# Masks of the transposed attention scores: added by VectorE in PSUM in place of matmuls with an identity

## The chip, the cores and the metric

The kernel runs on one core of one Trainium2 chip. The metric is the device time of one execution in microseconds (us); smaller is better. A "profile" here is one execution recorded by the hardware profiler: its span runs from the first to the last instruction that it lists.

## The reference, cut to what matters

One layer of a hybrid decoder trunk over 1024 tokens, 1024 wide, in float32. The input is normalised and projected once; four head groups of 256 channels work on the projection: sparse attention with three branches (NSA), differential attention, retention, and a Mamba-2 scan. Their outputs are gated, concatenated and projected back. The change touches the two attentions, whose scores are masked before the exponential:

```
def masked_softmax(s, mask):
    s = jnp.where(mask, s, -jnp.inf)
    m = jnp.max(s, axis=-1, keepdims=True)
    p = jnp.exp(s - jnp.where(jnp.isfinite(m), m, 0.0))
    return p / jnp.maximum(jnp.sum(p, axis=-1, keepdims=True), 1e-30)
...
dist = tb[:, None] - tk[None, :]                        # differential attention, per 128 queries
p = masked_softmax(s - slopes * dist, dist >= 0)         # causal
...
mask = (dist >= 0) & (dist < WINDOW) & (tk[:, None, :] >= 0)   # NSA window branch, WINDOW = 512
```

## The kernel before, in words

All matmuls of the projections and of the attention split one operand into a high and a low part (float32r) and accumulate several products in PSUM. `proj_t` (lines 267 to 269) and `proj_n` (283 to 285) issue three matmuls per block of 128 inputs; `weights` loads and splits the weights (254 on ScalarE, 187 in `low` on GpSimd).

Each attention head is computed twice over 512 queries (u = 0, 1). A first pass has queries on partitions: `diff_rows` and `nsa_rows` compute score tiles (helper `scores`, line 173), `Stats.tile` adds the mask and takes the maximum on VectorE in place in PSUM (476; 474 without a mask), ScalarE takes the exponential and the sum (477), and `Stats.shifts` and `rows` turn the sums into one shift per query, which is stored as extra rows of the query operand. A second pass has keys on partitions: `diff_out` and `nsa_out` compute the transposed scores, which now come out already shifted. For each block kb of 128 keys the score tile `S` is one or two matmuls (173 and, for NSA, 1079). Where the block meets the diagonal, or in the window branch its far edge, a 128-column mask is added. In the kernel before this is one more matmul into the same accumulation: the identity in bf16 as weights, the mask in bf16 (0 or -3e38) as the moving operand. It stands at line 582 in `score_t` (differential attention, tiles wider than 256 columns, one per softmax map), at 621 in `diff_out` (both maps in one tile of 2 x 256, the mask repeated for both), and at 1083 in `nsa_out` (one branch in a tile, or two narrow branches in one tile, again repeated). Then ScalarE takes the exponential from PSUM (`e`, lines 631, 623, 1088), the probabilities are split (`pth`, `ptl`: 589 and 592 in `pv`, 1090 to 1094 in `nsa_out`), and two matmuls multiply them with V into `O` (593, 594, 1098).

PSUM tiles come from rings: three buffers `S` for all score tiles, one `O`, two `mm` for projections, two `R` for the rest:

```
PSB = dict(S=3, O=1, mm=2, R=2)
```

Three streams of work are written as generators, each of whose steps issues a few instructions: `attention`, `recurrent` (`ssd_group`, `ret_pair`) and `projections`, which ends with `ssm_rows`, `ret_rows`, `gated`, `out_partial` (1203 to 1205, 1225) and `out_final`. `merge` picks the next step by weights (attention 400, recurrence 70, projections 660); attention and recurrence are lifted in priority. A scheduler then fixes every engine's order at build time, by priority and by its own estimate of when an instruction can start; on the chip each engine runs its list in that order.

```
att_, rec_ = lifted(attention(), PRIO), lifted(recurrent(), PRIO)
merge((att_, W_ATT), (rec_, W_REC), (proj, W_PROJ))
```

Of the kernel before, what the change touches and what calls it, by code (L numbers as in the profile page):

```python
# [15 lines left out]
ALU = mybir.AluOpType  # L16
# [6 lines left out]
P = 128  # L23
# [100 lines left out]
def hybrid_trunk_kernel(ctx: ExitStack, tc: tile.TileContext, a, out, dbg=None):  # L124
    nc = tc.nc
    V, A, T, G, SP = nc.vector, nc.scalar, nc.tensor, nc.gpsimd, nc.sync
# [14 lines left out]
    def sb(tag, shape, dt=F32):  # L141
        uid[0] += 1
        name = f"{tag}{uid[0]}"
        if tag == "w":
            return wpieces.pop(0)
        if tag in rings:
            return rings[tag].tile(shape, dt, name=name, padded_shape=[P] + list(shape[1:]))
        assert slots[tag], tag + " has no free slot"
        s = slots[tag].pop(0)
        t = s.tile(shape, dt, name=name)  # L150
        held[t.tensor.name] = (tag, s)
        return t

    def free(*tiles):
        for t in tiles:
            tag, s = held.pop(t.tensor.name)
            slots[tag].append(s)

    def const(name, shape, dt=F32):
        return pool.tile(shape, dt, name=name, tag=name, bufs=1)  # L160
# [4 lines left out]
    def ps(tag, shape):  # L165
        uid[0] += 1
        return psum.tile(shape, F32, name=f"{tag}{uid[0]}", tag=PMAP[tag], bufs=PSB[PMAP[tag]])
# [3 lines left out]
    def scores(tile_, *args, **kw):  # L171

        ins = T.matmul(tile_, *args, **kw)  # L173
        if kw["start"]:
            pace.append(ins)
# [18 lines left out]
    x = a["x"][0]  # L194
# [170 lines left out]
    m_causal_t, m_lower_t = [mk[:, i * P:(i + 1) * P] for i in (5, 6)]  # L365
    m_cmp = mk[:, 7 * P:7 * P + 512]
    ident_bf = const("ident_bf", [P, P], BF16)
# [42 lines left out]
    qa, ka, vd = {}, {}, {}  # L410
# [114 lines left out]
    def pair(m):  # L525

        return m[:, None, :].to_broadcast([P, 2, P])
# [12 lines left out]
    def diff_rows(h, u):  # L540
# [30 lines left out]
            move(qa[h, m][98:100, 512 * u:512 * u + 512], d_sd[h][u][2 * m:2 * m + 2, :])  # L571
        yield

    def score_t(s, w, parts, mask_lo, mask_hi):

        last = len(parts) - 1
        masks = [m for m in (mask_lo, mask_hi) if m is not None]
        for n, (k, q) in enumerate(parts):
            scores(s[:k.shape[-1], :q.shape[-1]], k, q, start=(n == 0), stop=(n == last and not masks))
        for n, (c, mk_) in enumerate(masks):  # L580
            kk = parts[0][0].shape[-1]
            T.matmul(s[:kk, c:c + mk_.shape[-1]], ident_bf[:kk, :kk], mk_, start=False, stop=(n == len(masks) - 1))

    def pv(o, e, vv, c0, w, first, last, hi_eng):

# [10 lines left out]
    def halves(dst, o):  # L596

        A.activation(dst, o[64:128, :], AF.Copy)
        V.tensor_tensor(dst, o[0:64, :], dst, op=ALU.add)

    def wide(q, lo, hi):

        a = min(lo, hi - 256)
        return q[:, a:hi], lo - a

    def diff_out(h, u):
        j, h2 = divmod(h, 2)
        if h2 == 0 and u == 0:
            y_diff[j] = sb("b", [P, S])
        o = ps("O", [P, 512])  # L610
        nk = 4 * u + 4
        for kb in range(nk):
            lo, hi = max(512 * u, kb * P), 512 * u + 512
            w = hi - lo
            es = []
            if w <= 256:
                s = ps("S", [P, 2, 256])
                for m in range(2):
                    q, x0 = wide(qa[h, m][0:100], lo, hi)
                    scores(s[:, m, :], ka[h, m][0:100, kb * P:kb * P + P], q, start=(m == 0), stop=False)  # L620
                T.matmul(s[:, :, x0:x0 + P], ident_bf, pair(m_causal_t), start=False, stop=True)
                e = sb("e", [P, 2, 256])
                A.activation(e[:, :, :w], s[:, :, x0:], AF.Exp)
                es = [e[:, 0, :w], e[:, 1, :w]]
            for m in range(2 if w > 256 else 0):
                s = ps("S", [P, 512])
                q, x0 = wide(qa[h, m][0:100], lo, hi)
                score_t(s, w, [(ka[h, m][0:100, kb * P:kb * P + P], q)],
                        (x0, m_causal_t) if kb * P >= 512 * u else None, None)
                e = sb("e", [P, 512])  # L630
                A.activation(e[:, :w], s[:, x0:x0 + w], AF.Exp)  # L631
                es.append(e[:, :w])
            V.scalar_tensor_tensor(es[0], es[1], neglam, es[0], op0=ALU.mult, op1=ALU.add)
            pv(o, es[0], vd[h][:, kb, :], lo - 512 * u, w, kb == 0, kb == nk - 1, A)
            yield
        halves(y_diff[j][64 * h2:64 * h2 + 64, 512 * u:512 * u + 512], o)
        yield
        if u:
            free(qa[h, 0], qa[h, 1], ka[h, 0], ka[h, 1], vd[h])
        if h2:  # L640
            diff_finish(j, u)
            yield
# [404 lines left out]
    def nsa_out(h, u):  # L1047
        hp, h2 = divmod(h, 2)
        if h2 == 0 and u == 0:
            y_nsa[hp] = sb("b", [P, S])  # L1050
        us = slice(512 * u, 512 * u + 512)
        o = ps("O", [P, 512])
        s = ps("S", [P, 2, P])
        for j in range(2):
            T.transpose(s[:, j, :], e_cmp[h, u][:, j, :], ident)
        hl = [sb(n, [P, 2, P], F32R) for n in ("pth", "ptl")]
        split(hl[0], hl[1], s)
        for a in range(2):
            for i in range(2):
                T.matmul(o[:, 256 * a:256 * a + 256], vvc[:, a, :], hl[i].rearrange("p j c -> p (j c)"),  # L1060
                         start=(a + i == 0), stop=False)
        yield
        groups, small = [], []
        for kb in range(4 * u + 4):
            for b in ("win", "slc"):
                lo, hi = max(512 * u, kb * P), 512 * u + 512
                edge = b == "win" and kb * P + 5 * P <= hi
                if edge:
                    hi = kb * P + 5 * P
                (small if hi - lo <= 256 else groups).append((b, kb, lo, hi, edge))  # L1070
        groups = [[g] for g in groups] + [small[i:i + 2] for i in range(0, len(small), 2)]
        for gi, g in enumerate(groups):
            wb = 256 if len(g) == 2 else 512
            s = ps("S", [P, len(g), wb])
            for j, (b, kb, lo, hi, edge) in enumerate(g):
                a0 = min(lo, hi - 256)
                scores(s[:, j, :hi - a0], k1[b][:, kb * P:kb * P + P], q1[h][:, a0:hi], start=(j == 0), stop=False)
                diag = kb * P >= 512 * u
                T.matmul(s[:, j, :hi - a0], k2[b][0:72, kb * P:kb * P + P], q2[h][0:72, a0:hi], start=False,
                         stop=not (edge or diag) and j == len(g) - 1)  # L1080
            for on, x, m in ((diag, lo - a0, m_causal_t), (edge, hi - a0 - P, m_lower_t)):
                if on:
                    T.matmul(s[:, :, x:x + P], ident_bf, m[:, None, :].to_broadcast([P, len(g), P]), start=False,  # L1083
                             stop=m is m_lower_t or not edge)
            xa, xb = min(e[2] - min(e[2], e[3] - 256) for e in g), hi - a0
            e, hl = sb("e", [P, len(g), wb]), [sb(n, [P, len(g), wb], F32R) for n in ("pth", "ptl")]
            e, hl = e[:, :, :xb - xa], [t[:, :, :xb - xa] for t in hl]
            A.activation(e, s[:, :, xa:xb], AF.Exp)  # L1088
            if gi % LO_POOL == LO_POOL - 1:
                A.activation(hl[0], e, AF.Copy)  # L1090
                G.tensor_tensor(hl[1], e, hl[0].bitcast(F32), op=ALU.subtract)
            else:
                G.tensor_scalar(hl[0], e, 1.0, 1.0, op0=ALU.mult, op1=ALU.mult)  # L1093
                V.tensor_tensor(hl[1], e, hl[0].bitcast(F32), op=ALU.subtract)  # L1094
            for j, (b, kb, lo, hi, edge) in enumerate(g):
                x = lo - min(lo, hi - 256) - xa
                for i, t in enumerate(hl):
                    T.matmul(o[:, lo - 512 * u:hi - 512 * u], vvs[b][:, kb, :], t[:, j, x:x + hi - lo], start=False,  # L1098
                             stop=(g is groups[-1] and j + i == 2))
            yield  # L1100
        halves(y_nsa[hp][64 * h2:64 * h2 + 64, us], o)
        yield
        if u:
            free(q1[h], q2[h])
            if h == 3:
                for b in ("win", "slc"):
                    free(k1[b], k2[b], vvs[b])
# [341 lines left out]
```

## Time and profile before

| what | value |
|---|---|
| three runs | 765.43, 770.51, 770.57 us; median 770.51 |
| profiled execution | 773.71 us, of it 771.9 us span |
| mean granted TensorE clock | 0.984 of full speed |
| TensorE busy (matmuls) | 727.9 us, 94% |
| TensorE weight loads | 591.7 us, 77%, beside the matmuls |
| VectorE busy | 509.2 us, 66%, 1452 instructions |
| ScalarE busy | 413.7 us, 54% |
| GpSimd busy | 305.3 us, 40% |

PE is TensorE's matmuls, PEld its weight loads, DVE is VectorE, ACT ScalarE, POOL GpSimd. A busy share is a mean over stages: what a stage costs is read from the stretch in which it stands. Successive matmuls overlap in the records, so the distance between their starts tells more than their length.

### The profile page before, as it was taken

What the parts mean: (1) busy time and instruction counts of PE and PEld (TensorE: products, weight loads), DVE (VectorE), ACT (ScalarE), POOL (GpSimd) and SP (SyncE); (2) the same over time, 40 slices, a digit from 0 to 9 for tenths busy, and PEclk for the clock granted to TensorE, in tenths of its full rate; (3) what the DMA queues carried; (4) which work ended last, traced back from release to release, by engine and by line L of the source; (5) the groups of instructions that cost most, each with busy time, mean ns of one, the idle gap of its engine ahead of it and who ended that gap; (6) DMA issues with size and microseconds to landing.
All of it is one profiled execution on the core that took longest, in us unless ns stands there. A gap on an engine that the chain in (4) does not pass through costs nothing.

```text
span 771.9 us, 12391 instructions
## 1 busy us (share of the span) xinstructions
PE 727.9 (94%) x3876; PEld 591.7 (77%) x3876; DVE 509.2 (66%) x1452; ACT 413.7 (54%) x1029; POOL 305.3 (40%) x476
## 2 busy tenths in 40 slices
PE   4999999999999999997999999999978999999994
PEld 4888777767787898775889888778866778788773
DVE  3752566444866856685696856657679897435587
ACT  6721566455667765473565544444446664454354
POOL 4231227111123115332442464456557752352446
PEclk9999999999999999999999999999987999999998
DMA  8548647755532533453232743225364223334365
GB/s 277 165 141 241 180 128 188 226 151 161 147 90 84 143 102 90 110 157 107 82 103 71 167 113 77 79 81 152 85 191 135 68 87 114 109 132 142 110 259 191
DMA packets 100845, 104.91 MB, mean 136 GB/s; under 512 B 15234, under 2 KB 76236, under 8 KB 100764
## 3 DMA queue, kind: packets, MB, share of 16 engines
q1 hardware_dynamic: 100684, 103.77, 45.8%
q8 instruction: 30, 0.49, 0.3%
q14 instruction: 35, 0.29, 0.2%
q0 software_dynamic: 96, 0.36, 0.1%
HBM read 71.91 MB, written 32.54 MB: 135 GB/s over the span
## 4 chain that ended last, share of the span: by engine, by line
PE 56%; DVE 14%; DMA 13%; issue 7%; POOL 5%; ACT 3%; SPq 1%; DVEq 0%; POOLq 0%; ACTq 0%
PE mm L267 7%; PE mm L268 7%; PE mm L269 7%; PE S L173 6%; DMA t<-d_cs 4%; PE mm L284 3%; PE mm L283 3%; PE mm L285 3%; PE O L1098 2%; DMA wraw<-in_w_in_dram 2%; POOL wlo L187 2%; DMA b<-in_w_in_dram 2%; DVE ptl L1094 2%; PE R L943 1%; PE mm L1203 1%
## 5 line engine op out<-in xcount | busy, mean ns | idle before, releaser
L187 POOL TENSOR_TENSOR wlo<-wraw,whi 128x256 fp32r<-128x256 f32 x132 | 99.3, 782 | 178.9 <-ACT whi L254 150.0
L267 PE MATMUL mm<-h,whi 128*128 128x512 f32 x400 | 161.9, 406 | 0.7 <-ACT ev L292 0.4
L268 PE MATMUL mm<-h,wlo 128*128 128x512 f32 x400 | 160.5, 401 | 0.0
L269 PE MATMUL mm<-h,whi 128*128 128x512 f32 x400 | 160.0, 400 | 0.0
L477 ACT ACTIVATE S<-S,sj 128x512 f32<-128x512 f32 (+3 forms) x192 | 103.7, 540 | 89.4 <-DVE sj L476 65.7
L173 PE MATMUL S<-b,b 100*128 100x256 f32 (+5 forms) x384 | 132.2, 366 | 6.7 <-ACT S L477 4.5
L476 DVE CUSTOM_DVE_ANT_0 S<-S,mk 128x512 f32<-128x512 f32 (+3 forms) x144 | 70.3, 495 | 40.5 <-PE S L173 17.1
L173 PEld LDWEIGHTS S<-b,b 100*128 100x128 f32 (+1 forms) x384 | 72.3, 192 | 23.7 <-ACT S L477 8.5
L267 PEld LDWEIGHTS mm<-h,whi 128*128 128x128 f32 x400 | 76.1, 190 | 16.2 <-ACT ev L292 0.6
L269 PEld LDWEIGHTS mm<-h,whi 128*128 128x128 f32 x400 | 75.9, 190 | 15.1
L268 PEld LDWEIGHTS mm<-h,wlo 128*128 128x128 f32 x400 | 75.9, 190 | 14.3 <-POOL wlo L187 0.4
L1093 POOL TENSOR_SCALAR pth<-e 128x512 fp32r<-128x512 f32 (+2 forms) x64 | 38.9, 613 | 56.3 <-ACT e L1088 25.8
L283 PE MATMUL mm<-whi,h 128*128 128x256 f32 (+1 forms) x192 | 55.8, 292 | 0.6 <-DVE ssmb L679 0.6
L1094 DVE TENSOR_TENSOR ptl<-e,pth 128x512 fp32r<-128x512 f32 (+2 forms) x64 | 45.7, 722 | 15.9 <-POOL pth L1093 13.4
L284 PE MATMUL mm<-wlo,h 128*128 128x256 f32 (+1 forms) x192 | 55.8, 293 | 0.0
L1088 ACT ACTIVATE e<-S 128x512 f32<-128x512 f32 (+2 forms) x76 | 40.3, 542 | 26.2 <-PE S L1083 14.7
L285 PE MATMUL mm<-whi,h 128*128 128x256 f32 (+1 forms) x192 | 54.2, 288 | 0.0
L254 ACT ACTIVATE whi<-wraw 128x1024 fp32r<-128x1024 f32 x29 | 30.6, 1055 | 24.4 <-DMA wraw<-in_w_in_dram 23.3
L474 DVE TENSOR_REDUCE sj<-S 128x1 f32<-128x512 f32 x48 | 32.6, 684 | 15.5 <-PE S L173 12.4
L631 ACT ACTIVATE e<-S 128x512 f32<-128x512 f32 (+1 forms) x64 | 35.7, 568 | 12.7 <-PE S L173 8.4
L778 DVE SCALAR_TENSOR_TENSOR t<-t,ncs,t 128x128 f32<-128x128 f32 x32 | 14.1, 475 | 38.8 <-POOL t L775 38.7
L477 ACT ACTIVATION_READ_ACCUMULATOR S<-S,sj 128x1 f32 x192 | 37.8, 197 | 0.0
(325 smaller groups left out, 1710.6 us busy)
## 6 DMA issues: line engine op xcount, KB each, us to landing
wraw<-in_w_in_dram SPq DMA_DIRECT2D x27, 512.0 KB
b<-in_x_dram SPq DMA_DIRECT2D x8, 512.0 KB
t<-d_cs SPq DMA_DIRECT2D x32, 128.0 KB
wraw<-in_w_out_dram SPq DMA_DIRECT2D x16, 256.0 KB
ev<-in_x_dram SPq DMA_DIRECT2D x16, 256.0 KB
d_part<-ev SPq DMA_DIRECT2D x16, 256.0 KB
b<-d_part SPq DMA_DIRECT2D x8, 512.0 KB
out_dram<-b SPq DMA_DIRECT2D x16, 256.0 KB
```

Source lines behind the costliest of these rows:

```text
L173: ins = T.matmul(tile_, *args, **kw)
L187: G.tensor_tensor(dst[:, cs], src[:, cs], hi[:, cs].bitcast(F32), op=ALU.subtract)
L267: paced(T.matmul(p, w[k][0], h_hi[k][:, hs], start=(k == 0), stop=False))
L268: T.matmul(p, w[k][1], h_hi[k][:, hs], start=False, stop=False)
L269: T.matmul(p, w[k][0], h_lo[k][:, hs], start=False, stop=(k == NK - 1))
L283: paced(T.matmul(p, h_hi[k][:, hs], w[k][0], start=(k == 0), stop=False))
L284: T.matmul(p, h_hi[k][:, hs], w[k][1], start=False, stop=False)
L285: T.matmul(p, h_lo[k][:, hs], w[k][0], start=False, stop=(k == NK - 1))
L476: V.tensor_tensor_reduce(s, s, bound, -1.0, -NEG, ALU.add, ALU.min, nm)
L477: A.activation(s, s, AF.Exp, bias=nm, scale=1.0 if bound is None else -1.0, accum_out=self.d[:, b, i, c:c + 1])
L1088: A.activation(e, s[:, :, xa:xb], AF.Exp)
L1094: V.tensor_tensor(hl[1], e, hl[0].bitcast(F32), op=ALU.subtract)
```

## The change

The 108 matmuls with the identity, and their weight loads, are gone. The last score matmul closes the accumulation (`stop`), and VectorE adds the mask to the tile in PSUM in place, before ScalarE reads it. Nothing else is edited; `nsa_rows` keeps its own mask matmul at line 988 and `ident_bf` with it.

```
+    def masked(s, m):
+        V.tensor_tensor(s, s, m, op=ALU.add)
...
     def score_t(s, w, parts, mask_lo, mask_hi):
         last = len(parts) - 1
-        masks = [m for m in (mask_lo, mask_hi) if m is not None]
         for n, (k, q) in enumerate(parts):
-            scores(s[:k.shape[-1], :q.shape[-1]], k, q, start=(n == 0), stop=(n == last and not masks))
-        for n, (c, mk_) in enumerate(masks):
-            kk = parts[0][0].shape[-1]
-            T.matmul(s[:kk, c:c + mk_.shape[-1]], ident_bf[:kk, :kk], mk_, start=False, stop=(n == len(masks) - 1))
+            scores(s[:k.shape[-1], :q.shape[-1]], k, q, start=(n == 0), stop=(n == last))
+        for c, mk_ in (m for m in (mask_lo, mask_hi) if m is not None):
+            masked(s[:parts[0][0].shape[-1], c:c + mk_.shape[-1]], mk_)
...
-                    scores(s[:, m, :], ka[h, m][0:100, kb * P:kb * P + P], q, start=(m == 0), stop=False)
-                T.matmul(s[:, :, x0:x0 + P], ident_bf, pair(m_causal_t), start=False, stop=True)
+                    scores(s[:, m, :], ka[h, m][0:100, kb * P:kb * P + P], q, start=(m == 0), stop=(m == 1))
+                masked(s[:, :, x0:x0 + P], pair(m_causal_t))
...
-                         stop=not (edge or diag) and j == len(g) - 1)
+                         stop=j == len(g) - 1)
             for on, x, m in ((diag, lo - a0, m_causal_t), (edge, hi - a0 - P, m_lower_t)):
                 if on:
-                    T.matmul(s[:, :, x:x + P], ident_bf, m[:, None, :].to_broadcast([P, len(g), P]), start=False,
-                             stop=m is m_lower_t or not edge)
+                    masked(s[:, :, x:x + P], m[:, None, :].to_broadcast([P, len(g), P]))
```

In the lists of the engines' orders, a name is a program name with the number of its tile; lines are those of the kernel listed. On TensorE, at the first masked tile of the differential attention (head 0, first half, `S_1348`), the difference of the two orders reads (- before only):

```order
 L269 MATMUL mm_1279<-h_164,whi_1272 128x512
 L173 MATMUL S_1348<-b_849,b_850 128x512
-L582 LDWEIGHTS ident_bf
-L582 MATMUL S_1348<-mk,ident_bf 128x128
 L267 MATMUL mm_1279<-h_157,whi_1272 128x512
 L268 MATMUL mm_1279<-h_157,wlo_1273 128x512
```

The load of the identity and the mask are gone; the projection matmuls around the score keep their places.

On VectorE, at the same place, while the shifts of another tile (`sj_1068`, the `Stats.shifts` of the second half) are worked out, the order before is:

```order
L492 TENSOR_TENSOR sj_1068<-sj_1068 128x16
L493 TENSOR_TENSOR sj_1068<-sj_1068 128x8
L496 TENSOR_SCALAR sj_1068<-sj_1068 128x8
L443 CAST sj_1068<-sj_1068 128x8
L444 TENSOR_SCALAR sj_1068<-sj_1068 128x8
L446 TENSOR_TENSOR sj_1068<-sj_1068 128x8
L447 TENSOR_SCALAR sj_1068<-sj_1068 128x8
L448 RECIPROCAL sj_1068<-sj_1068 128x8
L449 SCALAR_TENSOR_TENSOR sj_1068<-sj_1068 128x8
L633 SCALAR_TENSOR_TENSOR e_1351<-e_1356,lam,e_1351 128x512
```

And of the changed kernel, where line 576 is the new addition and 635 is the former 633:

```order
L576 TENSOR_TENSOR S_1348<-S_1348,mk 128x128
L492 TENSOR_TENSOR sj_1068<-sj_1068 128x16
L493 TENSOR_TENSOR sj_1068<-sj_1068 128x8
L496 TENSOR_SCALAR sj_1068<-sj_1068 128x8
L443 CAST sj_1068<-sj_1068 128x8
L444 TENSOR_SCALAR sj_1068<-sj_1068 128x8
L446 TENSOR_TENSOR sj_1068<-sj_1068 128x8
L576 TENSOR_TENSOR S_1353<-S_1353,mk 128x128
L447 TENSOR_SCALAR sj_1068<-sj_1068 128x8
L448 RECIPROCAL sj_1068<-sj_1068 128x8
L449 SCALAR_TENSOR_TENSOR sj_1068<-sj_1068 128x8
L450 TENSOR_TENSOR sj_1068<-sj_1068 128x8
```

The additions for the two maps now stand among the small steps of the statistics, and the combination of the two maps comes behind both.

Late in the program, on VectorE, where the second half of the SSM rows is normalised (`h_7057`, `sm_7062`) and the window and compressed scores of later NSA heads are on their way, the order before is:

```order
L1165 SCALAR_TENSOR_TENSOR h_6097<-PT_6981,vec,h_6096 128x512
L998 TENSOR_REDUCE sj_7198<-S_7227 128x4
L476 ISA S_7260,sj_7198<-S_7260,mk 128x128
L476 ISA sj_7198 128x1
L231 TENSOR_SCALAR sm_6871<-sm_6871 128x2
L231 TENSOR_SCALAR sm_7062<-sm_7062 128x4
```

And of the changed kernel (lines behind 577 are one or two higher than before: 1129 is the former 1128, 1166 the former 1165, 1157 the former 1156):

```order
L576 TENSOR_TENSOR S_7133<-S_7133,mk 128x128
L859 TENSOR_REDUCE sm_6871<-u_6870 128x2
L488 TENSOR_TENSOR sj_6558<-sj_6558 128x12
L231 TENSOR_SCALAR sm_7062<-sm_7062 128x4
L1129 SCALAR_TENSOR_TENSOR ev_6997<-PT_6992,wret,ev_6997 128x512
L231 TENSOR_SCALAR sm_6871<-sm_6871 128x2
L489 TENSOR_SCALAR sj_6558<-sj_6558 128x12
L576 TENSOR_TENSOR S_7180<-S_7180,mk 128x128
L1166 SCALAR_TENSOR_TENSOR h_6097<-PT_6981,vec,h_6096 128x512
L490 TENSOR_TENSOR sj_6558<-sj_6558 128x24
L1157 TENSOR_TENSOR h_7057<-h_7057,sm_7062 128x1024
```

Two additions stand between the steps that make the SSM rows ready for the output projection, and the normalisation of these rows comes earlier against the statistics of the attention.

## Rows read from the trace of the kernel before

**Rows 1.** The page, busy time: us, share of the span, instructions.

```profile
PE 727.9 (94%) x3876; PEld 591.7 (77%) x3876; DVE 509.2 (66%) x1452; ACT 413.7 (54%) x1029; POOL 305.3 (40%) x476
```

**Rows 2.** Busy time by stretch: length, engines, then clock, DMA share, GB/s.

```profile
0.00:325.00 325.00, 310.33 (x1636) 251.97 (x1637) 195.38 (x572) 185.67 (x446) 94.50 (x151) 1.00 0.55 156
325.00:375.00 50.00, 43.90 (x215) 34.52 (x214) 33.39 (x100) 25.81 (x63) 17.10 (x29) 0.97 0.43 116
375.00:550.00 175.00, 173.54 (x1015) 145.06 (x1014) 122.59 (x396) 90.19 (x232) 82.98 (x142) 1.00 0.38 102
550.00:650.00 100.00, 89.96 (x485) 72.12 (x484) 87.57 (x254) 56.93 (x160) 58.05 (x90) 0.93 0.38 117
650.00:775.00 125.00, 110.16 (x533) 88.00 (x532) 70.32 (x134) 55.06 (x130) 52.65 (x66) 0.96 0.42 152
```

**Rows 3.** The same view, engines PE PEld DVE ACT POOL, two shorter stretches.

```profile
571.50:594.00 22.50, 18.45 (x75) 13.68 (x75) 22.26 (x62) 14.74 (x43) 16.95 (x26) 0.70 0.59 185
612.50:637.00 24.50, 22.59 (x142) 18.77 (x142) 23.84 (x68) 15.39 (x43) 13.26 (x19) 1.00 0.33 106
```

**Rows 4.** Groups by line and shape: the mask matmuls; count, busy us, mean ns.

```profile
L1083 PE MATMUL S<-mk,ident_bf 128*128 128x128 bf16 x40 | 9.3, 233 | 0.0
L582 PE MATMUL S<-mk,ident_bf 128*128 128x128 bf16 x32 | 7.4, 231 | 0.0
L1083 PE MATMUL S<-mk,ident_bf 128*128 128x256 bf16 x20 | 5.5, 284 | 0.0
L621 PE MATMUL S<-mk,ident_bf 128*128 128x256 bf16 x16 | 4.5, 284 | 0.0
```

**Rows 5.** Timeline of TensorE around two masks: start us, length us, instruction.

```profile
112.95 0.23 PE L582 MATMUL S<-mk,ident_bf 128*128 128x128 bf16 x1
112.99 0.48 PE L267 MATMUL mm<-h,whi 128*128 128x512 f32 x1
113.30 0.39 PE L268 MATMUL mm<-h,wlo 128*128 128x512 f32 x1
113.54 0.39 PE L269 MATMUL mm<-h,whi 128*128 128x512 f32 x1
...
186.84 0.28 PE L621 MATMUL S<-mk,ident_bf 128*128 128x256 bf16 x1
186.88 0.48 PE L268 MATMUL mm<-h,wlo 128*128 128x512 f32 x1
187.19 0.39 PE L269 MATMUL mm<-h,whi 128*128 128x512 f32 x1
```

**Rows 6.** Mask matmuls by stretch (PE, PEld): lines 582, 621, then 1083 thrice.

```profile
325.00:375.00 50.00, 1.39 (x6) 0.58 (x6) 0.97 0.43 116
325.00:375.00 50.00, 1.14 (x4) 0.39 (x4) 0.97 0.43 116
550.00:650.00 100.00, 4.23 (x17) 1.62 (x17) 0.93 0.38 117
571.50:594.00 22.50, 0.80 (x3) 0.34 (x3) 0.70 0.59 185
612.50:637.00 24.50, 1.49 (x6) 0.58 (x6) 1.00 0.33 106
```

**Rows 7.** Groups by line and shape: VectorE's bounded maximum in PSUM, two widths.

```profile
L476 DVE CUSTOM_DVE_ANT_0 S<-S,mk 128x128 f32<-128x128 f32 x44 | 12.9, 293 | 9.8 <-PE S L1034 6.1 <-PE S L173 1.5 <-ACT S L477 1.4
L476 DVE CUSTOM_DVE_ANT_0 S<-S,mk 128x256 f32<-128x256 f32 x28 | 11.9, 427 | 5.8 <-ACT S L477 2.7 <-PE S L1034 2.2 <-PE S L173 0.5
```

**Rows 8.** Waits of all engines: waited for; us in total, times, longest.

```profile
ACT S L477 <- DVE sj L476: 65.7, 69, 3.7
```

**Rows 9.** Waits of TensorE alone.

```profile
PE S L173 <- ACT S L477: 4.5, 5, 2.5
PE O L1098 <- DVE ptl L1094: 2.8, 6, 0.8
```

**Rows 10.** Timeline of TensorE: one matmul and the idle time before it.

```profile
571.55 0.33 PE L994 MATMUL S<-tri,t 128*128 128x128 f32 x1 [2.66 <-ACT t L990]
```

## The prediction

> **What bounds the kernel now.** I read the share of busy time first, then the busy time by stretch, then what TensorE waits for, then the two stretches where it waits most, and last the single instructions that the change swaps. TensorE is busy 727.9 of the 771.9 us span, VectorE 509.2 [rows 1]. By stretch the picture splits [rows 2]: up to 325 us TensorE works 310.33 of 325 us (most of what is missing is the start), from 375 to 550 us 173.54 of 175, with VectorE at 60 to 70%. There, time is TensorE's own work, and what another engine does beside it is covered. From 325 to 375 us TensorE works 43.90 of 50 and from 550 to 650 us 89.96 of 100; in the latter VectorE works 87.57. Inside it are two pieces, 571.5 to 594 and 612.5 to 637 us, where VectorE is full (22.26 of 22.50 and 23.84 of 24.50) while TensorE is not (18.45 and 22.59) [rows 3]. I read these 47 us as VectorE's: by the code, the last recurrence chunks, the rows of the SSM and retention outputs, the statistics of the next attention rows and the split of the probabilities come together there, and the partial output projection, which would fill TensorE, starts only behind them. After 650 us TensorE works 110.16 us again and VectorE 70.32 [rows 2]; the end is the tail of the final normalisation, which the change does not touch.
>
> **What goes from TensorE.** The removed instructions are 32 + 16 in the differential attention and 40 + 20 in the NSA attention: 72 over 128 columns and 36 over 256, each with its own weight load of the identity [rows 4]. Their durations (231 to 284 ns) overlap with their neighbours, so what counts is how far one moves the next starts. Matmuls of 512 columns normally start 0.23 to 0.24 us apart (113.30 to 113.54). After a 128-column mask the second matmul starts at 113.30 instead of 112.95 + 0.23 = 113.18: the mask costs 0.12 us. After a 256-column mask it starts at 187.19 instead of 186.84 + 0.23 = 187.07: again 0.12 us [rows 5]. So all 108 take 108 x 0.12 = 13.0 us of TensorE, and this is the most the removal can give.
>
> [...]
>
> What of this lies on the path? Of the 108, 6 + 4 stand between 325 and 375 us and 17 between 550 and 650 us, 3 and 6 of them in the two pieces that VectorE fills [rows 6]. The other 108 - 10 - 17 = 81, and the 8 of the 17 outside the two pieces, stand where TensorE is the longest: 89 x 0.12 = 10.7 us gained. The 9 in the full pieces gain nothing, since TensorE waits there anyway.
>
> **What comes to VectorE.** 108 in-place additions, PSUM and a bf16 mask to PSUM. The trace has no plain one, but VectorE's bounded maximum of line 476 reads a score tile in PSUM and a bf16 mask and writes the tile back: 293 ns for 128 columns, 427 for 256 [rows 7]. I take these: 72 x 0.293 + 36 x 0.427 = 36.5 us, VectorE at 545.7 us in all, still below TensorE's 714.9.
> - In the dense stretches (81 of them, some 27 us) the additions run beside projection matmuls. I cost them at nothing: VectorE has 30 to 40% free there. Were that cover gone, each would show with its whole 0.34 us on average.
> - In the two full pieces they cost their duration. By the times of before 9 masks fall there, two of them wide (1.49 us for the second piece's six is 4 x 0.233 + 2 x 0.284 [rows 4, 6]): 7 x 0.293 + 2 x 0.427 = 2.9 us. By the instruction order of the changed program, 18 additions (12 narrow, 6 wide) stand on VectorE between the first gated row and the first partial output: 12 x 0.293 + 6 x 0.427 = 6.1 us. I take the middle, 4.5.
> - Between 325 and 375 us ten masks come: 6 x 0.293 + 4 x 0.427 = 3.5 us of VectorE in a stretch where it is 67% busy and TensorE idles 6.1 us. At worst all 3.5 show; at best the ten matmuls gain 10 x 0.12 = 1.2. I take 1.0 lost, nearer to the gain, since VectorE is not full.
>
> **The added hop.** Exp now waits for VectorE instead of TensorE, so one of the three S buffers stays taken longer, and behind a waiting addition on VectorE stand the small statistics and the split of the probabilities, for which TensorE's products with V wait. The nearest thing in the trace is the row path: 144 tiles go TensorE, VectorE (line 476), ScalarE (line 477) through the same three buffers. ScalarE waited 65.7 us for VectorE on this path [rows 8], yet TensorE waited only 4.5 us for a buffer, and 2.8 us for the split [rows 9]: 4.5 / 144 = 0.03 us a tile. For 108 tiles that would be 3.4 us, but most of the 4.5 lies in the full pieces, which are already counted; I take 0, with 0 and 3.4 as ends.
>
> No DMA is added, removed or newly waited for: SyncE's list holds the same transfers in nearly the same order. The order on TensorE keeps its pattern, masks taken out, with products with V and recurrence steps a few matmuls earlier or later.
>
> **Sum.** -10.7 + 4.5 + 1.0 + 0 = -5.2 us. The profiled execution took 773.7 us, so 768.5; it lies 3.2 us above the median of the runs shown, 770.5. From the median the forecast is 765.3 us, 0.7% faster. A difference under 1% (7.7 us) is about what a measurement of this kernel cannot tell from none, so the likeliest verdict is "within 1%".
>
> **Rivals.**
> 1. *All of TensorE's gain is kept.* VectorE's pieces are full because work is queued, not because it must all be done there: after the pieces, from 650 us on, VectorE is busy for little more than half of the time [rows 2], and additions could displace work that nobody waits for. Then the 89 give 10.7, the ten 1.2: 770.5 - 11.9 = 758.6 us. Against it: VectorE is busy 97 to 99% in the pieces [rows 3], and attention, with its masks, has the higher priority in the order. It is faster by over 1% as soon as the two VectorE losses together stay below 3.0 us.
> 2. *VectorE's queue becomes the wait.* One mechanism: the addition stands in program order behind whatever VectorE does, so a masked tile holds its S buffer for its own 0.34 us plus one VectorE instruction (509.2 us / 1452 = 0.35 us), 0.69 us more, and TensorE, whose order is fixed, stands at the next score matmul. If that shows for every third mask, 36 x 0.69 = 24.8 us against 13.0 gained: 770.5 + 11.8 = 782.3 us. It decides from 13.0 / 108 = 0.12 us a mask for no gain, and from (13.0 + 7.7) / 108 = 0.19 us a mask for slower by 1%. For it: the 65.7 us of ScalarE's waits. Against it: TensorE's 0.03 us a tile. [...]
> 3. *Gain and loss cancel.* The full pieces take all 6.1, the stretch from 325 us all 3.5: -10.7 + 9.6 = -1.1, 769.4 us. Within 1%, as the forecast.
>
> **How the numbers follow.** Forecast and rival 3 together 0.48, rival 1 0.31, rival 2 0.21. Rival 1's end with everything hidden is -13.0 us, 757.5; below that I see nothing. Above, 779 leaves out somewhat over half of rival 2, under 0.2. Faster by over 1% is below 762.8, slower above 778.2.
>
> **What would show it.** Right: 108 fewer matmuls on TensorE, its busy time down by 8 to 13 us; 108 VectorE additions near 0.29 and 0.43 us; TensorE as dense as before up to 325 us and from 375 to 550 us, with the score's next stages some 10 us earlier by 550 us; and the 47 us of VectorE's pieces grown by 3 to 6. Wrong: TensorE's waits for ScalarE's exp or for the split of the probabilities grown by 10 us or more, a drop of the granted clock in a stretch that was dense, additions that take much over 0.45 us, or the full pieces not longer at all.

## The result, and the profile after

The changed kernel takes 759.03 us (median of four runs, 757.33 to 764.18) against 770.54 us of the kernel before in the same comparison: a ratio of 0.985, with a 95% interval of 0.982 to 0.989. It is faster by 1.5%, and the interval lies wholly below 1. The forecast was 765.3 us and "within 1%"; the measured time is that of rival 1 (758.6 us). The experiments below show a second thing: the 1.5% belongs to one instruction order, and four other orders of the same instructions do not have it. One profiled execution among them (the kernel before at weight 655) ran at a mean granted clock of 0.845 and took 797.02 us, so its parts are not used.

The page of the changed kernel, busy times over a span of 757.1 us (before: [rows 1]):

```profile
PE 715.2 (94%) x3768; PEld 591.7 (78%) x3768; DVE 528.9 (70%) x1560; ACT 415.0 (55%) x1029; POOL 312.6 (41%) x476
```

108 matmuls fewer and 108 VectorE instructions more, as the diff says. TensorE is busy 12.7 us less, VectorE 19.7 us more. Its additions, as groups by line and shape (count, busy us, mean ns, then the idle time before them):

```profile
L576 DVE TENSOR_TENSOR S<-S,mk 128x128 f32<-128x128 f32 x72 | 20.8, 292 | 10.6 <-PE S L173 6.2 <-PE S L1081 3.8
L576 DVE TENSOR_TENSOR S<-S,mk 128x256 f32<-128x256 f32 x36 | 15.4, 431 | 7.1 <-PE S L1081 5.6 <-ACT u L837 0.8 <-PE S L173 0.4
```

292 and 431 ns, beside the 293 and 427 ns that were assumed from the bounded maximum [rows 7]: 36.2 us in all. VectorE's busy time has grown by only 19.7 us, though: successive records overlap on VectorE too. Before, the durations of its 1452 instructions add up to 590.4 us at a busy time of 509.2; after, those of 1560 add up to 618.7 at 528.9. So the overlap grew by 8.6 us (81.2 to 89.8), and the durations of the 1452 other instructions add up to some 8 us less than before (618.7 less 36.6 for the additions, beside 590.4). By stretch (length, the engines in the order of the page, clock, DMA share, GB/s; before: [rows 2]):

```profile
0.00:325.00 325.00, 308.93 (x1624) 254.95 (x1625) 205.64 (x613) 189.84 (x455) 97.46 (x154) 1.00 0.55 156
325.00:375.00 50.00, 47.99 (x241) 39.88 (x241) 37.13 (x128) 27.47 (x68) 18.57 (x32) 0.97 0.48 131
375.00:550.00 175.00, 172.42 (x999) 146.52 (x997) 130.37 (x412) 91.78 (x236) 89.36 (x146) 1.00 0.42 114
550.00:650.00 100.00, 91.93 (x469) 73.60 (x470) 85.14 (x267) 56.22 (x157) 57.23 (x85) 0.95 0.35 107
650.00:775.00 125.00, 93.94 (x440) 76.75 (x438) 70.64 (x143) 49.70 (x115) 49.93 (x63) 0.95 0.38 135
```

The stretch from 325 to 375 us, for which a loss of 1.0 us was forecast, is denser than before: TensorE idles 50 - 47.99 = 2.0 us there in place of 6.1. Two landmarks say more than fixed times. The last projection matmul (line 267) starts at 544.6 us, before at 568.0: 23.4 us earlier. Up to there TensorE has this behind it, first of the kernel before, then of the changed one:

```profile
0.00:568.03 568.03, 545.62 (x2963) 446.33 (x2964) 362.44 (x1098) 309.06 (x761) 201.47 (x335) 1.00 0.48 135
0.00:544.62 544.62, 525.23 (x2842) 438.83 (x2843) 368.70 (x1138) 304.26 (x744) 200.91 (x324) 1.00 0.50 140
```

Of the 121 matmuls fewer, 69 are masks (32 of line 582, 16 of 621, 21 of 1083); the other 52 (net) have moved behind the last projection matmul. The second landmark is the 24th matmul at the former line 1203. (By the code each tile of the output projection has six of them, so 24 are four tiles; the expectations below call this place the eighth output tile.) It starts at 633.2 us, before at 646.6: 13.4 earlier, so the late stretch between the two has grown by 10.0 us. From there to the end it is 123.9 us, before 125.3. The late stretch, in the same columns, of the kernel before:

```profile
568.00:646.60 78.60, 68.75 (x366) 54.46 (x365) 73.19 (x209) 48.60 (x136) 51.04 (x76) 0.91 0.36 112
```

and of the changed kernel:

```profile
544.60:633.20 88.60, 79.27 (x413) 62.31 (x412) 81.53 (x260) 54.55 (x154) 58.37 (x85) 0.94 0.35 106
```

It is longer because more of the program stands in it, 413 matmuls in place of 366, and TensorE works 10.5 us more; it idles 9.3 us in it, before 9.9. VectorE is 92% busy in it, before 93%, with 17 of the additions (5.8 us) among its work. So TensorE's waiting in the stretch that VectorE nearly fills did not grow under the additions.

For an account of the whole span I take three parts from the profile: TensorE's idle time (span less busy time), the half-clock loss (half of TensorE's busy time in stretches with a granted clock of 0.5), and the rest, its work at full clock. The half is an estimate: in the changed kernel's stretch at 346 us below, matmuls of 512 columns start 0.43 us apart, just ahead of it 0.23. The second part comes from the stretches with a clock of 0.5. Of the kernel before they are:

```profile
351.50:354.90 3.40, 3.40 (x10) 2.63 (x10) 1.92 (x3) 0.61 (x2) 2.62 (x4) 0.50 0.03 12
573.40:587.00 13.60, 10.82 (x34) 7.83 (x33) 13.50 (x38) 7.83 (x25) 11.32 (x18) 0.50 0.79 251
764.50:771.90 7.40, 0.00 (x0) 0.00 (x0) 3.24 (x4) 1.18 (x3) 3.01 (x4) 0.50 0.55 208
```

and of the changed kernel:

```profile
346.20:349.60 3.40, 3.40 (x10) 2.60 (x9) 1.33 (x4) 1.97 (x4) 0.67 (x1) 0.51 0.64 171
551.00:561.20 10.20, 9.18 (x35) 7.80 (x36) 9.40 (x31) 5.37 (x17) 9.16 (x14) 0.50 0.64 202
714.90:718.30 3.40, 3.40 (x11) 2.83 (x12) 3.03 (x6) 1.99 (x4) 1.55 (x3) 0.50 0.00 0
749.00:757.10 8.10, 0.00 (x0) 0.00 (x0) 3.24 (x4) 1.27 (x3) 3.10 (x4) 0.50 0.51 194
```

Before, (3.40 + 10.82) / 2 = 7.1 us are lost to the clock; after, (3.40 + 9.18 + 3.40) / 2 = 8.0.

| us | span | work at full clock | half-clock loss | idle |
|---|---|---|---|---|
| before | 771.9 | 720.8 | 7.1 | 44.0 |
| after | 757.1 | 707.2 | 8.0 | 41.9 |
| difference | -14.8 | -13.6 | +0.9 | -2.1 |

In these two executions the saved work is all kept. They differ by more than the medians, 14.9 us beside 11.5, since that of the kernel before lies 3.2 us above its median; by the medians 2.1 of the 13.6 us came back. One execution's waiting is thus known to a few us only (the kernel before took 767.61 to 773.57 us in 25 runs of one comparison). Waits of all engines (waited for; us in total, times, longest): ScalarE's wait for VectorE on the row path is 48.5 us, before 65.7 [rows 8], and 32.9 us of waits for the additions have come beside it:

```profile
ACT S L477 <- DVE sj L476: 48.5, 55, 4.1
ACT e L1089 <- DVE S L576: 19.8, 19, 2.8
ACT e L633 <- DVE S L576: 8.6, 15, 1.6
ACT e L625 <- DVE S L576: 4.5, 5, 2.0
```

The largest of TensorE's own waits for a score buffer and for the split probabilities are 3.2 and 4.0 us, before 4.5 and 2.8 [rows 9]; with all smaller ones of either kind they are 3.8 and 5.1, before 4.7 and 5.1:

```profile
PE O L1099 <- DVE ptl L1095: 4.0, 7, 1.3
PE S L173 <- ACT S L477: 3.2, 4, 1.6
```

### The profile page after: what moved, and what is told of

It is laid out like the page before. It is cut to its first block, busy times and chain, and to the rows that moved or that the text cites. A ratio compares the mean times of both kernels' runs of the same rounds, so it can differ in the third digit from the quotient of the medians.

```text
span 757.1 us, 12299 instructions
## 1 busy us (share of the span) xinstructions
PE 715.2 (94%) x3768; PEld 591.7 (78%) x3768; DVE 528.9 (70%) x1560; ACT 415.0 (55%) x1029; POOL 312.6 (41%) x476
## 4 chain that ended last, share of the span: by engine, by line
PE 63%; DMA 14%; DVE 11%; POOL 5%; issue 3%; ACT 2%; SPq 1%; DVEq 0%; POOLq 0%; ACTq 0%
PE mm L267 9%; PE mm L269 9%; PE mm L268 9%; PE S L173 7%; DMA t<-d_cs 4%; PE O L1099 3%; PE mm L284 2%; PE mm L283 2%; PE mm L285 2%; DMA b<-in_w_in_dram 2%; PE mm L1206 1%; PE mm L1204 1%; PE mm L1205 1%; PE S L1081 1%; PE R L945 1%
## 5 line engine op out<-in xcount | busy, mean ns | idle before, releaser
L477 ACT ACTIVATE S<-S,sj 128x512 f32<-128x512 f32 (+3 forms) x192 | 103.4, 539 | 75.7 <-DVE sj L476 48.5
L173 PE MATMUL S<-b,b 100*128 100x256 f32 (+5 forms) x384 | 130.5, 363 | 4.5 <-ACT S L477 3.2
L268 PEld LDWEIGHTS mm<-h,wlo 128*128 128x128 f32 x400 | 75.9, 190 | 14.9
L576 DVE TENSOR_TENSOR S<-S,mk 128x128 f32<-128x128 f32 (+1 forms) x108 | 36.2, 339 | 17.7 <-PE S L1081 9.4
L474 DVE TENSOR_REDUCE sj<-S 128x1 f32<-128x512 f32 x48 | 32.6, 684 | 15.1 <-PE S L173 10.5
L232 POOL TENSOR_TENSOR sm<-sm,mhalf 128x2 f32<-128x2 f32 (+3 forms) x30 | 25.9, 864 | 31.6 <-DVE sm L231 24.2
```

Source lines behind the costliest of these rows:

```text
L268: T.matmul(p, w[k][1], h_hi[k][:, hs], start=False, stop=False)
L477: A.activation(s, s, AF.Exp, bias=nm, scale=1.0 if bound is None else -1.0, accum_out=self.d[:, b, i, c:c + 1])
```

## Experiments

Ratios are to the kernel before, measured in the same comparison, with the 95% interval. "Waiting" is idle time plus half-clock loss of the profiled execution.

**What the parts cost.** The first theory (A): the time follows TensorE's work, 0.12 us a mask. Its rivals: the additions cost something of their own, or the new order does.

*No masks at all* (line numbers of the changed kernel; the three exponentials get a scale of zero to keep their input finite):

```
     def masked(s, m):
-        V.tensor_tensor(s, s, m, op=ALU.add)
+        pass
...
-                A.activation(e[:, :w], s[:, x0:x0 + w], AF.Exp)
+                A.activation(e[:, :w], s[:, x0:x0 + w], AF.Exp, scale=0.0)
```

> Leaves out the masks of the transposed scores: no mask matmul and no addition (the exponential takes scale 0 so that the numbers stay finite; its size is unchanged). Theory A (TensorE's work alone sets the time and VectorE's additions are hidden everywhere): the same as the changed kernel, 11 to 13 us under before. Theory B (the additions cost some 5 us in the stretch where VectorE is full, and something else made that good): 16 us or more under before, that is 4 to 6 us under the changed kernel. Theory C (a large part of the 11.5 us is the luck of the scheduler's order): anything, with TensorE's idle time and not its busy time making the difference.

Measured: 773.88 us, ratio 1.003 [1.000, 1.006]. TensorE's work is as low as in the changed kernel (706.7 us), yet it is 15 us slower: the waiting is 61.6 us in place of 49.9, in an execution of 770.11 us. A and B missed; C is nearest, with 5.8 us more idle time and 5.9 more half-clock loss than the changed kernel. The page:

```profile
PE 720.7 (94%) x3768; PEld 597.4 (78%) x3768; DVE 503.5 (66%) x1452; ACT 412.4 (54%) x1029; POOL 314.2 (41%) x476
```

*Both* (the mask matmuls of the kernel before, and after each an addition of zeros; at 621 and 1083 likewise):

```
             T.matmul(s[:kk, c:c + mk_.shape[-1]], ident_bf[:kk, :kk], mk_, start=False, stop=(n == len(masks) - 1))
+        for c, mk_ in masks:
+            zeros_added(s[:parts[0][0].shape[-1], c:c + P])
```

> The kernel before with its 108 mask matmuls, and 108 VectorE additions of zeros to the same columns behind them: the hop and VectorE's 36 us alone, with nothing saved on TensorE. Theory A: within 2 us of before. Theory B: 5 to 10 us slower than before (4.5 in VectorE's full pieces, up to 3.5 between 325 and 375 us, and the longer hold of the S buffers). Theory C: a shift of several us either way, seen as idle time of TensorE at places without masks.

Measured: 787.67 us, ratio 1.021 [1.014, 1.027]; work 718.5, idle 48.2, half-clock loss 22.0 us. It is slower by more than any of the three expected.

*Each mask matmul twice* (kernel before, an identity times zeros ahead of each mask):

```
+            T.matmul(s[:kk, c:c + P], ident_bf[:kk, :kk], mk[:, P:2 * P], start=False, stop=False)
             T.matmul(s[:kk, c:c + mk_.shape[-1]], ident_bf[:kk, :kk], mk_, start=False, stop=(n == len(masks) - 1))
```

> The kernel before with every mask matmul preceded by one more of the same shape that adds zeros: the price of the 108 matmuls by itself, in the other direction. Theory A: TensorE's busy time up by 12 to 14 us and the time up by 10 to 13 us (108 at 0.12, less those where TensorE waits anyway). Theory B: the same, 10 to 11 us. Theory C: busy time up by 12 to 14 us, but the time by clearly less or more than 10 to 13.

Measured: 773.46 us, ratio 1.003 [1.001, 1.005]; work 724.7 us, 3.9 more than before for 108 more masks, and busy time 3.0 more, where all three theories had 12 to 14. TensorE's timeline at the two places of [rows 5] (start, length, instruction):

```profile
111.57 0.23 PE L582 MATMUL S<-mk,ident_bf 128*128 128x128 bf16 x1
111.64 0.22 PE L583 MATMUL S<-mk,ident_bf 128*128 128x128 bf16 x1
111.66 0.48 PE L267 MATMUL mm<-h,whi 128*128 128x512 f32 x1
111.98 0.39 PE L268 MATMUL mm<-h,wlo 128*128 128x512 f32 x1
...
186.70 0.28 PE L622 MATMUL S<-mk,ident_bf 128*128 128x256 bf16 x1
186.82 0.27 PE L623 MATMUL S<-mk,ident_bf 128*128 128x256 bf16 x1
186.85 0.48 PE L268 MATMUL mm<-h,wlo 128*128 128x512 f32 x1
187.17 0.34 PE L594 MATMUL O<-pth,b 128*128 128x384 f32 x1
```

From the first mask of 128 columns to line 268 it is 0.41 us, with one mask 0.35 [rows 5]: the second mask costs 0.06 us, the first 0.12. At 256 columns it is 0.47 us beside 0.35: there the second costs 0.12 us, like the first. By these prices 108 second masks would take 72 x 0.06 + 36 x 0.12 = 8.6 us; the other 4.7 us did not show in the work, which differs by 3.6 us between the orders of the kernel before in the next experiment.

*Each addition twice* (changed kernel, a second addition of zeros):

```
         V.tensor_tensor(s, s, m, op=ALU.add)
+        z = mk[:, P:2 * P] if len(s.shape) == 2 else mk[:, None, P:2 * P].to_broadcast([P, s.shape[1], P])
+        V.tensor_tensor(s, s, z, op=ALU.add)
```

> The changed kernel with a second addition, of zeros, behind every addition: VectorE's 36 us once more. Theory A: within 2 us of the changed kernel, until VectorE (some 565 us busy) becomes the longest somewhere. Theory B: 5 to 10 us slower than the changed kernel, and VectorE's late stretch longer by that. Theory C: a shift of several us either way without VectorE being full where it arises.

Measured: 788.52 us, ratio 1.022 [1.019, 1.025]; work 709.8, idle 54.1, half-clock loss 23.8 us. This too is slower than any of the three expected.

Theory A falls: two kernels with the least work are 15 us apart, and additions of zeros bring 17 us to the kernel before and 29 to the changed one. But each edit also gave the scheduler another program and so another order on every engine. Is it the edit that the time follows, or the order?

**The same instructions in other orders.** One number is changed, in either kernel: the projections' weight in `merge`, to 655, 665, 650 and 670. No instruction is added or removed.

```
-W_ATT, W_REC, W_PROJ = 400, 70, 660
+W_ATT, W_REC, W_PROJ = 400, 70, 655
```

> The kernel before with the projections' weight in the merge of the streams at 655 instead of 660: the same instructions in another order on every engine. Theory A (work alone decides): within 3 us of before. Theory C (the order of the moment decides as much as the change): TensorE's full-clock work as before (720.8 us), but idle time and half-clock loss, 44.0 + 7.1 us in before, differing by 5 us or more.

> The changed kernel with that weight at 655. Theory A: 11 to 14 us under the same weight's kernel with mask matmuls. Theory B: 5 to 9 us under it. Theory C: TensorE's full-clock work 13 to 14 us under it, and the difference of the times anywhere from -25 to +5 us, since idle time and half-clock loss fall out anew.

> The kernel before with that weight at 665. As for 655: theory A within 3 us of before, theory C a difference of 5 us or more, all of it in TensorE's idle time and half-clock loss, none in its full-clock work.

> The changed kernel with that weight at 665. As for 655: theory A 11 to 14 us under the same weight's kernel with mask matmuls, theory B 5 to 9 us, theory C full-clock work 13 to 14 us under it and the time anywhere from -25 to +5 us.

> The kernel before with the projections' weight at 650, one more order of the same instructions. Theory D (formed after the runs so far: the removal always takes some 13 us off TensorE's work, and VectorE's additions make TensorE's idle time and half-clock loss larger by an amount that depends on the order, on average about as much): idle time plus half-clock loss 44 to 54 us, as in the orders of before seen so far (51.1 and 52.2 us), so 763 to 774 us. Theory C (pure luck of the order, the same spread with and without additions): idle time plus loss anywhere from 45 to 75 us.

> The changed kernel at 650. Theory D: TensorE's full-clock work 706 to 709 us, idle time plus half-clock loss 50 to 76 us (as the three orders so far: 49.9, 60.1 and 75.6), most of the excess between the end of the projections and the eighth output tile; 757 to 785 us. Theory A: 11 to 14 us under the kernel of the same weight with mask matmuls.

> The kernel before at 670. Theory D: idle time plus half-clock loss 44 to 54 us, 763 to 774 us. Theory C: anywhere from 45 to 75 us.

> The changed kernel at 670. Theory D: full-clock work 706 to 709 us, idle time plus half-clock loss 50 to 76 us, most of the excess between the end of the projections and the eighth output tile. Theory A: 11 to 14 us under the kernel of the same weight with mask matmuls.

Measured:

| weight | before, us | ratio | after, us | ratio | after less before |
|---|---|---|---|---|---|
| 650 | 767.94 | 0.997 [0.994, 1.000] | 769.76 | 0.999 [0.995, 1.002] | +0.2% |
| 655 | 765.28 | 0.992 [0.988, 0.995] | 782.80 | 1.013 [1.007, 1.018] | +2.1% |
| 660 | 770.54 | 1 | 759.03 | 0.985 [0.982, 0.989] | -1.5% |
| 665 | 771.62 | 0.999 [0.997, 1.001] | 772.08 | 1.001 [0.998, 1.004] | +0.2% |
| 670 | 769.91 | 0.999 [0.995, 1.002] | 771.15 | 1.003 [1.000, 1.006] | +0.4% |

The five differences have a mean of +0.3% and a standard deviation of 1.3%, so the mean is known to about 0.6% (1.3% over the root of 5): it is not told apart from zero, nor from the forecast's -0.7%. The parts, without those of 655 before:

| weight | work before | after | waiting before | after |
|---|---|---|---|---|
| 650 | 720.0 | 706.8 | 45.5 | 57.2 |
| 655 | | 706.2 | | 75.6 |
| 660 | 720.8 | 707.2 | 51.1 | 49.9 |
| 665 | 717.2 | 708.6 | 52.2 | 60.1 |
| 670 | 718.1 | 704.2 | 50.2 | 65.2 |

The work goes down in every pair (13.2, 13.6, 8.6 and 13.9 us). The waiting goes up by 11.7, 7.9 and 15.0 us in three of them (650, 665, 670), and down by 1.2 in the pair that was to be predicted (up by 2.1 by the medians). D's forecasts of the waiting at 650 and 670 were met, but not that most of the excess would stand in the late stretch: between the two landmarks the waiting changes by +3.4, -2.3 and +5.2 us in the three pairs, and the rest of the excess stands ahead of it and behind it. At 655 the difference of the times, +17.5 us, lies outside C's range too. The slowest, the changed kernel at 655, in its stretches at a clock of 0.5 (columns as above):

```profile
325.20:328.70 3.50, 3.50 (x10) 2.72 (x9) 2.47 (x9) 2.89 (x7) 1.68 (x3) 0.51 0.31 106
386.70:390.10 3.40, 3.24 (x13) 3.05 (x14) 1.90 (x5) 0.25 (x2) 1.49 (x3) 0.50 0.17 33
536.90:540.30 3.40, 3.18 (x14) 3.18 (x15) 2.24 (x9) 0.74 (x4) 2.26 (x4) 0.50 0.23 82
557.40:560.80 3.40, 3.40 (x12) 2.59 (x12) 3.33 (x11) 2.52 (x8) 1.77 (x4) 0.50 0.60 196
564.20:581.20 17.00, 15.89 (x59) 13.58 (x60) 14.35 (x50) 10.23 (x35) 13.03 (x20) 0.50 0.49 151
594.90:601.70 6.80, 6.55 (x20) 4.95 (x21) 5.47 (x22) 4.12 (x12) 3.61 (x5) 0.50 0.01 2
615.40:622.20 6.80, 6.80 (x22) 5.21 (x21) 4.41 (x13) 2.90 (x8) 6.28 (x10) 0.50 0.00 0
```

TensorE is busy 42.56 us in them: 21.3 us lost, in place of 8.0 at 660. Its six largest waits between 230 and 660 us end with six different releasers, none of them an addition:

```profile
PE mm L267 <- DVE ev L745: 2.9, 1, 2.9
PE O L1099 <- POOL pth L1094: 2.8, 3, 1.8
PE R L765 <- ACT t L519: 2.3, 1, 2.3
PE S L173 <- ACT S L477: 2.3, 5, 0.9
PE S L173 <- DVE ce L1003: 2.2, 1, 2.2
PE R L843 <- DVE t L797: 2.1, 1, 2.1
```

By itself this does not clear the additions, since ScalarE's exponential stands between an addition and TensorE. Over the whole program TensorE's waits for a score buffer and for the split add up to 14.1 us, at 660 to 8.9 (3.8 + 5.1). But the longest of those for a buffer (2.2 us, until 202.8 us, behind the exponential of line 625) goes back to ScalarE's wait for a weight transfer (the brackets show the wait before the instruction):

```profile
201.25 1.06 ACT L254 ACTIVATE whi<-wraw 128x1024 fp32r<-128x1024 f32 x1 [3.56 <-DMA wraw<-in_w_in_dram]
```

**Removal or additions?** Two theories for the waiting that comes back. D: the additions cause it, so that without any masks it stays as low as before. E: the removal causes it, since work taken from TensorE leaves it waiting for the same chains of the other engines. The kernels without masks and with both, as above, at 655 and 665:

> Leaves out the masks of the transposed scores (neither matmuls nor additions; the exponential takes scale 0), at weight 655. Theory D (the additions cause the extra idle time and half-clock loss): full-clock work 704 to 709 us, idle time plus loss 44 to 54 us, so 752 to 763 us. Theory E (the removal itself turns into waiting): idle time plus loss 55 to 66 us, as in the same kernel at 660 (61.6), so 763 to 774 us.

> Mask matmuls kept and zeros added by VectorE behind each, at weight 655. Theory D: full-clock work 717 to 721 us, idle time plus half-clock loss 55 to 76 us as in the kernels with additions, so 775 to 797 us. Theory E (the additions cost nothing of themselves): idle time plus loss 44 to 54 us, so 764 to 775 us.

> As the kernel without masks at 655, at weight 665 (it leaves out the masks of the transposed scores). Theory D: idle time plus loss 44 to 54 us, 752 to 763 us; theory E: 55 to 66 us, 763 to 774 us.

> As the kernel with both at 655, at weight 665. Theory D: idle time plus loss 55 to 76 us, 775 to 797 us; theory E: 44 to 54 us, 764 to 775 us.

Measured, waiting in us at weights 655, 660, 665, and the median times:

| kernel | waiting | times, us | ratios |
|---|---|---|---|
| before | -, 51.1, 52.2 | 765.3, 770.5, 771.6 | 0.992, 1, 0.999 |
| no masks | 57.8, 61.6, 59.2 | 762.5, 773.9, 766.8 | 0.988 [0.985, 0.992], 1.003, 0.995 [0.992, 0.997] |
| after | 75.6, 49.9, 60.1 | 782.8, 759.0, 772.1 | 1.013, 0.985, 1.001 |
| both | 45.6, 70.2, 50.7 | 767.9, 787.7, 768.9 | 0.995 [0.993, 0.997], 1.021, 0.997 [0.994, 1.000] |

Without any mask instruction TensorE waits 57.8 to 61.6 us, more than the 45.5 to 52.2 of the kernel before in the four orders that have parts. Their mean is 59.5 us beside 49.8, so 9.8 us of the saved work come back as waiting (5.4 idle, 4.4 half-clock loss) although VectorE has nothing more to do. That is E's result in all three orders, though the time at 655, 762.5 us, lies in D's range. With both mask and addition, the waiting is as E has it at 655 and 665, and as high as D has it at 660. D's share stays open. Averaged over the three orders, the additions cost 771.3 - 767.7 = 3.6 us beside no masks and 774.8 - 769.1 = 5.7 us beside the kernel before, with signs that differ from order to order.

**The late additions.** Theory D, now for one place: the additions that stand where VectorE is nearly full (the late stretch) are what slows the changed kernel at 655. Of the 20 additions there, 15 belong to the NSA attention of head 1, second half, and head 2, first half; made matmuls again, they should give the time back:

```
+        on_pe = (h, u) in ((1, 1), (2, 0))
...
-                if on:
+                if on and on_pe:
+                    T.matmul(s[:, :, x:x + P], ident_bf, m[:, None, :].to_broadcast([P, len(g), P]), start=False,
+                             stop=m is m_lower_t or not edge)
+                elif on:
```

> The changed kernel at weight 655, but the 15 masks of the NSA tiles of head 1, second half, and head 2, first half, which fall into the late stretch, are matmuls again. Theory D (the additions there make that stretch long): the stretch back from 103.9 to 82 to 92 us, the time from 782.8 to 765 to 772 us. Theory E (the order as a whole): the stretch and the time fall anywhere among the orders seen, 82 to 104 us and 759 to 783 us, with no bond to the 15 masks.

> The same at weight 660, the changed kernel's own. Theory D: the late stretch shorter than the changed kernel's 88.6 us by about VectorE's 5 us, the time 753 to 758 us, under both kernels. Theory E: the changed kernel's 759.0 us is a good draw among orders, and a new order most likely falls behind it: 762 to 775 us.

Measured: at 655 782.98 us, ratio 1.014 [1.008, 1.020], beside 1.013 with all masks on VectorE; at 660 762.53, 0.989 [0.982, 0.995], beside 0.985. The late stretch (between the two landmarks) at 655, of the changed kernel:

```profile
557.50:661.40 103.90, 95.04 (x455) 76.27 (x454) 91.28 (x296) 60.70 (x172) 58.22 (x90) 0.84 0.30 91
```

and with the 15 late masks on TensorE:

```profile
557.40:656.60 99.20, 90.97 (x469) 72.65 (x468) 89.44 (x281) 60.32 (x174) 59.46 (x91) 0.88 0.31 97
```

The stretch gets 4.7 us shorter, where D had 12 us or more, and the end is where it was; at 660 the stretch is 89.2 us beside 88.6, and the time is E's. D is not supported here. But this edit is a new order as well, so it does not rule out a share of these 15 additions. No kernel that computes the masks beat the changed kernel at 660.

## Why the prediction was right or wrong

- **What goes from TensorE: right.** 108 x 0.12 = 13.0 us was forecast, the work fell by 13.6 in this pair and by 8.6 to 13.9 in all four pairs that have parts. That 19 of the masks stand where TensorE waits anyway took 2.3 us off; by the medians 2.1 us came back as waiting, by the two profiles nothing.
- **The additions' durations: right; VectorE's time for them: too high.** 36.2 us measured, 36.5 forecast, but VectorE's busy time is 528.9 us and not 545.7: it grew by 19.7 us, 0.18 an addition in place of 0.34, with 8.6 us more overlap among VectorE's records and some 8 us less in the durations of its other instructions. The forecast took overlap into account for TensorE's matmuls, but not here. In the dense stretches the additions are hidden: up to 325 us and from 375 to 550 us TensorE idles 16.1 + 2.6 us, before 14.7 + 1.5.
- **VectorE's full pieces (4.5 us) and 325 to 375 us (1.0 us): wrong for this order, and the step that put the forecast within 1%.** These 5.5 us were charged, and TensorE's waiting as a whole changed by -1.2 us (profiles) to +2.1 us (medians). TensorE idles 9.3 us in the late stretch, before 9.9, though 17 additions stand there, and 4.1 us less between 325 and 375 us. The forecast charged VectorE's added busy time to the pieces of before, as if the same work met again there. But the projections ended 23.4 us earlier, and the late stretch holds 413 matmuls in place of 366.
- **"The order on TensorE keeps its pattern": wrong, and the deeper fault.** At one masked tile it was true in the two orders. Over the program it was not: 52 matmuls (net) that are no masks moved behind the last projection matmul. And the order counts: the same instructions in five orders take 765.3 to 771.6 us (before) and 759.0 to 782.8 us (after). That spread of up to 23.8 us is larger than each term of the sum. A range of one kernel's rows could not see it.
- **The hop (0): right in this order.** ScalarE waits 32.9 us for the additions and 17.2 us less on the row path; TensorE's waits for a buffer and for the split change by -0.9 and 0.0 us.
- **Rival 1** gave the time, and its reason (additions displace work that nobody waits for) fits the account of this pair, but was not tested by itself. **Rival 2** (VectorE's queue becomes the wait, 782.3 us) did not happen at 660. At 655 the time is 782.8, by its mechanism at most in part: TensorE's waits for a buffer and for the split are 5.2 us more than at 660 (14.1 - 8.9), of 25.7 us more waiting, and 13.3 us of it (21.3 - 8.0) is half-clock loss.

So the 1.5% is real for this pair, and its account is that of rival 1. That the saving was kept in this pair is luck of the order: with the masks left out altogether at the same weight, TensorE has as little work, and the time is 14.9 us longer. That the edit as such makes the kernel faster is not shown: over five orders the saved 8.6 to 13.9 us of work mostly became waiting, and the mean difference is +0.3% with an uncertainty of 0.6%. Not tried: one fixed order for both kernels, and other work put into TensorE's pauses. Which chain of the other engines holds the removal's gain back was not isolated either.

## What to carry to other kernels

Where a scheduler fixes the order at build time, every edit is also a new order: build the kernel before and after in several orders that change nothing else (here one weight), and compare the scatter with the effect before giving the effect a cause. Split the span into TensorE's work at full clock, half-clock loss and idle time; a change that removes work is worth only what does not reappear in the other two. In these orders most of it did.

## What the hardware showed that was not expected

- At the two places of [rows 5] a lone bf16 matmul between float32 matmuls costs 0.12 us, at 128 columns as at 256; in the kernel with each mask twice, a second one behind it costs 0.06 us at 128 columns and 0.12 at 256.
- Records of VectorE's instructions overlap, by 81.2 us before and 89.8 after in sum. With additions of 0.29 and 0.43 us its busy time is up by 0.18 us for each on average in this pair, 0.15 to 0.21 in the three others (16.2, 20.2 and 23.2 us for 108).
- In these traces the length of a pause of TensorE does not tell how long a granted clock of 0.5 follows it. The 2.66 us pause that ends at 571.55 us in the kernel before [rows 10] is followed, from 573.4 us on, by 13.6 us at a clock of 0.5 (with another pause, of 2.53 us, in them), one of 2.67 us in the same kernel by 3.4 us, and one of 2.90 us in the changed kernel at 655 by none: the granted clock is 1.00 from there to 386.7 us.

```profile
351.29 0.35 PE L173 MATMUL S<-b,k1c 128*128 128x256 f32 x1 [2.67 <-DMA b<-d_nq]
350.60 0.51 PE L267 MATMUL mm<-h,whi 128*128 128x512 f32 x1 [2.90 <-DVE ev L745]
```

- In the kernel without masks at 655, one pause of 5.36 us (TensorE's timeline: start, length, instruction, the wait before it)

```profile
559.12 0.55 PE L1062 MATMUL O<-pth,vvc 128*128 128x256 f32 x1 [5.36 <-ACT h L1130]
```

and a second one, of 2.6 us, stand in a stretch of 27.3 us at a clock of 0.5 (windows, columns as above), in which TensorE works 19.52 us and so loses some 9.8:

```profile
553.90:581.20 27.30, 19.52 (x66) 16.28 (x67) 20.44 (x65) 12.02 (x38) 12.44 (x23) 0.50 0.43 132
```

- In the kernels of this study the half-clock loss ranges from 4.8 us (before, 650) to 23.8 us (additions twice). From 650 to 670, with the changed kernel's instructions alone, it goes from 8.0 to 21.3 us, while its work at full clock stays within 704.2 to 708.6.
